# One plain chunk instead of two at the head of each feed-forward block, and a pair of chunks joined by TensorE in PSUM banks that ScalarE fills

## The chip, the cores and the metric

One core of one Trainium2 chip runs the whole program. TensorE multiplies into eight PSUM banks, VectorE, ScalarE and GpSimd work beside it, SP and GpSimd issue most of the DMAs. The metric is the device time of one execution in microseconds, before and after, over several runs.

## The reference

A trunk of two layers on two token batches (512 and 256 tokens, 768 in all, width 1024) with shared weights, in float32. Each layer adds half a feed-forward block, a token mixer (layer 0 a gated linear recurrence in both directions, layer 1 attention in a window of 128 tokens) and another half feed-forward block; a final norm closes it.

```python
def swiglu_ffn(x, w1, w2):
    gate, up = jnp.split(x @ w1, 2, axis=-1)
    return (jax.nn.silu(gate) * up) @ w2

for li in range(DEPTH):
    x = x + 0.5 * swiglu_ffn(rmsnorm(x, norm_g[li, 0]), ffn_w1[li, 0], ffn_w2[li, 0])
    h = rmsnorm(x, norm_g[li, 1])
    ...
    x = x + mix
    x = x + 0.5 * swiglu_ffn(rmsnorm(x, norm_g[li, 2]), ffn_w1[li, 1], ffn_w2[li, 1])
return rmsnorm(x, final_norm_g)
```

So there are four feed-forward blocks, f0 to f3. w1 is 1024 x 5632 (gate and up, 2816 columns each), w2 is 2816 x 1024.

## The kernel before, in words

**Number format.** Every float32 operand is split into a high part, rounded to the matmul format, and the low rest. A product is three matmuls: high by high, high by low, low by high. ScalarE makes the high part (L175, L208, L319), VectorE the low one by a subtraction (L176, L209, L320); in one product of each pair, p5, GpSimd makes the weight's low part (L209).

**Chunks.** The 2816 hidden columns are 22 chunks of 128. For a chunk the kernel needs the gate bank and the up bank for 768 tokens, and the tokens are handled in two halves of 384 (H). The inner size of 1024 is eight slices k, in two parts of four. The normalized, transposed tokens are held as operand tiles `b00`, `b10` (part 0 and 1 of half 0), `b01`, `b11` (half 1), split high and low.

**Plain chunks.** `up_plain` (L490) multiplies gate and up directly: for each of two banks and each half 8 k x 3 matmuls, through `mm3` (L312, its matmuls are L314 to L316), then silu on ScalarE (L504) and a multiplication on VectorE (L505).

**Pairs.** The other chunks take gate and up together as a 2 x 2 block matrix by 2 x 2 blocks of tokens, in seven products p1 to p7 instead of eight (the scheme of Strassen and Winograd). The weight blocks are a11, a12 (gate, part 0 and 1) and a21, a22 (up); sums of them are formed in place: a21 += a22 and a tile s3 = a21 + a11 by accumulating DMAs that GpSimd issues (L147), then "second" (a11 += a21) and "fourth" (a12 += a11) on VectorE (L215). The token side needs t1 to t4, differences of b00 to b11, made once a block by `sums` and `mix` (L420 to L442) and split by `put`. `FACTOR` names the token operand of each product: p1 takes b00, p2 b10, p3 b11, p4 t4, p5 t1, p6 t2, p7 t3. `product` (L508; the matmuls are L513) does 4 k x 3 matmuls into one bank; `up_pair` (L523) runs the seven into four banks a, b, c, d and joins them: ScalarE copies a and c out (L530, L533), VectorE does seven operations (L539 to L552), ScalarE the two silu.

**A block.** `ffn` (L601) works through `GROUPS` of four chunks. After four chunks the hidden values, in the same seven-product form (`gather`), go through `down_quad` (L556, matmuls L577), whose results are added to x on VectorE (L599). In the first group `PLAIN` chunks are plain, and between their matmuls stand calls of `run_later`, which run what is deferred: the two turns of half 1 (`turn`, transposes L385, copies L396, then `put`) and `sums`. Two remaining chunks are pairs whose hidden values go into the closing (the loop over `b` at the end of `ffn`, plain matmuls of 512 columns), where each block of 128 tokens is finished and normalized at once (`after_block`, `norm_block`) and half 0 is turned for the next stage. The stretch from a block's first plain matmul to its first product is called its opening here.

**Weights.** `plan_ffn` queues the weights. `load_next` issues the loads on SP's queue into `RAWBUFS` = 4 raw tiles; a pair also loads `s3` and starts its two accumulating DMAs on GpSimd's queue. `stage_next` makes one staged product (high and low) in the order `UP`; `WBUFS` = 8 staged tiles are there, a product of a pair takes one, a plain weight two. `ahead` stages as many as are free; `done` is release and ahead.

**Order.** A scheduler places the instructions: program order is the priority, and what is ready by its own cost model goes first on each engine; each engine then runs its list in order. `issue_after(x)` keeps what stands in its block behind x on the same engine.

Of the kernel before, what the change touches and what calls it, by code (L numbers as in the profile page):

```python
# [12 lines left out]
AF = mybir.ActivationFunctionType  # L13
# [3 lines left out]
P = 128  # L17
# [19 lines left out]
PLAIN = 2  # L37
# [6 lines left out]
UP = ("p1", "p7", "p2", "p5", "p4", "p6", "p3")  # L44
# [8 lines left out]
class Trunk:  # L53
    def __init__(self, ctx, tc, consts):
# [10 lines left out]
        self.uid = 0  # L65
        self.deferred = []
# [11 lines left out]
    def tmp(self, n, dt=F32):  # L78
        tag, bufs, size = ("tA", 8, TA) if n > TB else ("tB", 2, TB)
        t = self.tp.tile([P, size], dt, tag=tag, name=self.name(tag), bufs=bufs)  # L80
        return t[:, :n]

# [98 lines left out]
    def quad_steps(self, key, raws, srcs, order):  # L181
# [35 lines left out]
        behind = {"p5": "second", "p4": "fourth"} if up else {}  # L217
# [94 lines left out]
    def mm3(self, out, a, b, first, last):  # L312
# [3 lines left out]
        nc.tensor.matmul(out, a[1], b[0], start=False, stop=last)  # L316
# [122 lines left out]
    def sums(self):  # L439
        for kp in range(2):  # L440
            tiles = (self.tn[(i // 2, i % 2)][:, kp] for i in range(4))
            self.mix(*tiles, lambda name, src: self.put(name, kp, src))  # L442
# [27 lines left out]
    def plan_ffn(self, tag, w1, w2):  # L470
        def up(i):
# [4 lines left out]
            else:  # L476
                self.plan_quad((tag, i), (gate, up), (NC, P), UP)
# [12 lines left out]
    def up_plain(self, tag, j, half):  # L490
        pss = []
        for c in range(2):
            wh, wl = self.take((tag, j, c))
            ps = self.ps(H)
            for k in range(NC):
                b = self.operand(f"b{k // 4}{half}", k % 4)
                self.mm3(ps, (wh[:, k, :], wl[:, k, :]), b, k == 0, k == NC - 1)
                if half == 0 and k in (((), (2, 6)), ((3, 7), (3, 7)))[j][c]:
                    self.run_later()
            if half:  # L500
                self.done((tag, j, c))
            pss.append(ps)
        t = self.tmp(H)
        self.nc.scalar.activation(t, pss[0], AF.Silu)  # L504
        self.nc.vector.tensor_mul(t, t, pss[1])  # L505
        return t
# [16 lines left out]
    def up_pair(self, tag, j):  # L523
        nc = self.nc
        key = (tag, j)
        a, b, c, d = (self.ps(H) for _ in range(4))
        v, w, t = (self.tmp(H) for _ in range(3))
        p = lambda name, ps, first, last: self.product(key, name, FACTOR[name], ps, first, last)
        p("p1", a, True, False)
        nc.scalar.copy(v, a)  # L530
        self.ahead()
        p("p7", c, True, False)
        nc.scalar.copy(w, c)  # L533
        self.ahead()
        p("p2", a, False, True)
        nc.scalar.activation(a, a, AF.Silu)
        self.ahead()
        p("p5", d, True, False)
        nc.vector.tensor_sub(w, w, d)  # L539
        self.ahead()  # L540
        p("p4", c, False, True)
        p("p6", b, True, True)
        nc.vector.tensor_sub(v, v, b)
        nc.vector.tensor_sub(t, c, v)
        nc.vector.tensor_mul(t, t, a)  # L545
        yield t
        nc.vector.tensor_sub(w, w, v)
        self.ahead()
        p("p3", d, False, True)
        nc.vector.tensor_add(v, v, d)  # L550
        self.last_act = nc.scalar.activation(v, v, AF.Silu).ins
        self.last_dve = nc.vector.tensor_mul(w, v, w).ins  # L552
        yield w
        self.ahead()

    def down_quad(self, tag, g, hid):  # L556
        nc = self.nc
        cols = lambda b, c: self.x[b][:, c * 512 : (c + 1) * 512]
        if g == 0:
            for i in range(HB):  # L560
                x12, x21, x22 = cols(HB + i, 0), cols(i, 1), cols(HB + i, 1)
                nc.vector.tensor_add(x12, x12, x22)
                nc.vector.tensor_sub(x21, x21, x22)
# [37 lines left out]
    def ffn(self, tag, next_row):  # L601
        for g in range(GROUPS):
# [7 lines left out]
            def gather(ts, kp):  # L610
                self.mix(ts[0], ts[1], ts[2], ts[3], lambda name, src: put(name, src, kp))

            if g == 0:
                ts = {}
                for half in range(2):
# [944 lines left out]
```

## Time and profile before

| | before |
|---|---|
| time, median of 3 runs | 2768.38 us (2768.38 to 2769.55) |
| span of the profiled execution, first to last instruction | 2767.2 us |
| the profiled execution's own time by the page | the span; the median of the runs is 1.2 us longer |
| TensorE busy | 2745.0 us (99%), 15117 matmuls |
| VectorE busy | 2206.5 us (80%) |
| ScalarE busy | 1386.0 us (50%) |
| GpSimd busy | 453.0 us (16%) |
| mean granted TensorE clock | 0.999 |

The trace names instructions by engine (PE, PEld for weight loads, DVE for VectorE, ACT for ScalarE, POOL for GpSimd, SP) and by line of the kernel. The chain of waits follows the work that ended last back to what released it. In the groups, the numbers behind the bar are busy time, mean duration of one, and idle time just before them with what ended it. Durations of matmuls overlap: the distance from one to the next is read from a run of them in the chain. In a list in order of time the columns are start, duration, engine, line, operation, tiles; a bracket is idle time before it and what ended that.

### The profile page before, as it was taken

Reading aid. Unit: us, or ns where it says so; the run is one execution under the profiler, and the core shown is the slowest. Engines: PE = TensorE matmul, PEld = TensorE weight load, DVE = VectorE, ACT = ScalarE, POOL = GpSimd, SP = SyncE. Lnnn points to the kernel's source line nnn. Section 1 sums busy time; section 2 is a strip of 40 time slices with the busy share of each in tenths; the row PEclk is TensorE's granted clock in tenths of the full one; section 3 lists DMA queues with packets and bytes.
Section 4 is the critical chain, followed back from the end, with each engine's and each line's share of the span. In section 5 each row is a group of like instructions: output and inputs, shape, how many; then the busy total and the mean of one; then the engine's idle time right before and its main releaser. Section 6 shows DMA issues by size and latency. Waiting matters only on the chain.

```text
span 2767.2 us, 40933 instructions
## 1 busy us (share of the span) xinstructions
PE 2745.0 (99%) x15117; PEld 2554.8 (92%) x15117; DVE 2206.5 (80%) x3766; ACT 1386.0 (50%) x2589; POOL 453.0 (16%) x491
## 2 busy tenths in 40 slices
PE   8999999999999999999999999999999999999998
PEld 8999999989999889999999999999888889999998
DVE  8788788767887888788878887887847868788877
ACT  7344444634455675444445543444458855444443
POOL 2111121200000101211111121111105611211111
PEclk9999999999999999999999999999999999999999
DMA  6554554851122743655444355544424422655443
GB/s 172 130 125 114 126 140 124 227 161 39 39 62 66 205 119 78 143 134 131 115 117 121 78 145 134 126 119 118 130 73 111 89 69 73 145 134 130 114 118 107
DMA packets 352040, 325.22 MB, mean 118 GB/s; under 512 B 14216, under 2 KB 271200, under 8 KB 351840
## 3 DMA queue, kind: packets, MB, share of 16 engines
q1 hardware_dynamic: 303040, 224.56, 27.7%
q0 software_dynamic: 44496, 84.56, 17.4%
q10 hardware_dynamic: 4304, 13.49, 1.3%
q8 instruction: 118, 1.93, 0.3%
q14 instruction: 82, 0.67, 0.1%
HBM read 225.82 MB, written 15.73 MB: 87 GB/s over the span
## 4 chain that ended last, share of the span: by engine, by line
PE 96%; DVE 2%; ACT 1%; DMA 1%; issue 0%; DVEq 0%; POOL 0%; SPq 0%; ACTq 0%; POOLq 0%
PE ps L513 42%; PE ps L577 21%; PE ps L315 6%; PE ps L316 6%; PE ps L314 6%; PE ps L760 5%; PE ps L823 3%; PE ps L928 1%; PE ps L1414 1%; PE ps L904 1%; PE ps L385 1%; PE ps L1426 0%; PE ps L1376 0%; PE ps L1427 0%; PE ps L1377 0%; PE ps L1181 0%
## 5 line engine op out<-in xcount | busy, mean ns | idle before, releaser
L513 PE MATMUL ps<-big,w 128*128 128x384 f32 x6720 | 1169.3, 334 | 0.0
L513 PEld LDWEIGHTS ps<-big,w 128*128 128x128 f32 x6720 | 1165.9, 188 | 1.7 <-ACT tA L530 0.2
L208 ACT CAST w<-wr 128x512 fp32r<-128x512 f32 x600 | 415.8, 707 | 689.2 <-PE ps L513 274.9
L577 PE MATMUL ps<-w,big 128*128 128x512 f32 x2520 | 575.7, 390 | 0.0
L577 PEld LDWEIGHTS ps<-w,big 128*128 128x128 f32 x2520 | 472.7, 188 | 98.0 <-ACT big L319 0.4
L209 DVE TENSOR_TENSOR w<-wr,w 128x512 fp32r<-128x512 f32 (+1 forms) x520 | 438.0, 846 | 145.9 <-ACT w L208 123.9
L147 POOL DMA_DIRECT2D s<-wr x126 | 109.8, 878 | 1250.3 <-DMA s<-in_ffn_w_dram 432.0
L599 DVE SCALAR_TENSOR_TENSOR x<-ps,x 128x512 f32<-128x512 f32 x468 | 302.4, 686 | 10.1 <-PE ps L316 10.0
L314 PE MATMUL ps<-big,w 128*128 128x384 f32 x640 | 219.6, 345 | 1.2 <-ACT w L175 0.9
L315 PE MATMUL ps<-big,w 128*128 128x384 f32 x640 | 215.7, 337 | 0.7 <-DVE big L320 0.7
L316 PE MATMUL ps<-big,w 128*128 128x384 f32 x640 | 214.6, 335 | 0.0
L319 ACT CAST big<-tA 128x384 fp32r<-128x384 f32 x296 | 148.0, 513 | 115.4 <-DVE tA L545 37.0
L147 POOL DMA_DIRECT2D wr<-wr x109 | 94.9, 871 | 518.3 <-DMA wr<-in_ffn_w_dram 165.9
L760 PE MATMUL ps<-w,big 128*128 128x512 f32 x756 | 177.1, 392 | 0.1
L320 DVE TENSOR_TENSOR big<-tA,big 128x384 fp32r<-128x384 f32 x296 | 168.0, 578 | 6.7 <-ACT big L319 4.7
L209 POOL TENSOR_TENSOR w<-wr,w 128x512 fp32r<-128x512 f32 x80 | 137.4, 1718 | 197.8 <-ACT w L208 195.8
L760 PEld LDWEIGHTS ps<-w,big 128*128 128x128 f32 x756 | 140.6, 188 | 29.1 <-DVE w L320 0.6
L215 DVE TENSOR_TENSOR wr<-wr,wr 128x512 f32<-128x512 f32 (+1 forms) x120 | 123.3, 1027 | 25.9 <-issue 23.6
L314 PE MATMUL ps<-w,big 128*128 128x512 f32 x336 | 134.6, 401 | 0.1
L316 PE MATMUL ps<-w,big 128*128 128x512 f32 x336 | 131.8, 392 | 0.5 <-DVE big L400 0.5
L315 PE MATMUL ps<-w,big 128*128 128x512 f32 x336 | 131.8, 392 | 0.0
L315 PEld LDWEIGHTS ps<-big,w 128*128 128x128 f32 x640 | 120.6, 188 | 2.0 <-DVE big L320 1.7
(214 smaller groups left out, 3504.0 us busy)
## 6 DMA issues: line engine op xcount, KB each, us to landing
wr<-in_ffn_w_dram SPq DMA_DIRECT2D x264, 512.0 KB, 4.0
s<-wr POOLq DMA_DIRECT2D x126, 256.0 KB, 4.8
s<-in_ffn_w_dram SPq DMA_DIRECT2D x120, 256.0 KB, 3.2
wr<-wr POOLq DMA_DIRECT2D x80, 256.0 KB, 3.8
wr<-in_hg_w_in_dram SPq DMA_DIRECT2D x32, 512.0 KB, 3.9
wr<-wr POOLq DMA_DIRECT2D x29, 512.0 KB, 4.6
spill<-x ACTq DMA_DIRECT2D x12, 512.0 KB, 4.0
kept<-big POOLq DMA_DIRECT2D x8, 768.0 KB, 9.7
```

Of the source, the lines that this page charges most:

```text
L147: self.nc.gpsimd.dma_start(out, src, accum_op=ALU.add)
L208: nc.scalar.copy(h, src)
L209: (eng or nc.vector).tensor_sub(l, src, h.bitcast(F32))
L314: nc.tensor.matmul(out, a[0], b[0], start=first, stop=False)
L315: nc.tensor.matmul(out, a[0], b[1], start=False, stop=False)
L316: nc.tensor.matmul(out, a[1], b[0], start=False, stop=last)
L319: self.nc.scalar.copy(hi, src)
L320: self.nc.vector.tensor_sub(lo, src, hi.bitcast(F32))
L513: self.nc.tensor.matmul(ps, a[x], b[y], start=first and k == 0 and i == 0, stop=k == 3 and i == 2, skip_group_check=True,)
L577: nc.tensor.matmul(ps, a[x], w[y], start=name == chain and kp == 0 and q == 0, stop=kp == 1 and q == 2, skip_group_check=True,)
L599: self.nc.vector.scalar_tensor_tensor(x, ps, c, x, ALU.mult, ALU.add)
L760: nc.tensor.matmul(ps, x[:, sl], y, start=fresh and k == 0 and q == 0, stop=k == 3 and q == 2, skip_group_check=True,)
```

## The change

- `PLAIN` is 1: chunk 1 of each block becomes a pair. The groups stay five of four chunks, and the last two chunks stay pairs.
- The opening is put in a new order: the plain chunk's gate part 0 for half 0, p1 of chunk 1, up part 0, gate part 1, up part 1, p2 of chunk 1, then the plain chunk's half 1, then p5, p6, p3, p7 of chunk 1, p1 of chunk 2 and p4 of chunk 1. The plain parts of half 0 are kept in this order among themselves. The deferred steps stand behind gate part 1, up part 1 and p2. Chunk 1's weights are staged in the order `UP_OPEN`.
- A pair's sums are formed in PSUM: ScalarE writes -a into bank b before p6 adds to it, and b into bank c before p7 and p4 add to c. VectorE keeps four operations. The first such banks of a block are those that the plain chunk wrote (`wide`). In a pair half 1 is finished first and half 0 last.
- The weight's "second" is formed behind p1 and "fourth" behind p2.
- `sums` forms each token factor for both kp together, in the order t1, t2, t3, t4.
- The six additions of x ahead of the first `down_quad` are kept behind chunk 1's last VectorE operation.
- The closing starts with the first halves of three token blocks instead of two, and the staging of the next stage's weights that followed its last matmuls follows the whole loop.

```diff
-PLAIN = 2
+PLAIN = 1
...
-UP = ("p1", "p7", "p2", "p5", "p4", "p6", "p3")
+UP = ("p1", "p5", "p6", "p2", "p7", "p3", "p4")
+UP_OPEN = ("p1", "p2", "p5", "p6", "p3", "p7", "p4")
...
+    def seeded(self):
+        return self.wide.pop(0) if self.wide else self.ps(H)
...
-        behind = {"p5": "second", "p4": "fourth"} if up else {}
+        behind = {"p1": "second", "p2": "fourth"} if up else {}
...
     def sums(self):
-        for kp in range(2):
-            tiles = (self.tn[(i // 2, i % 2)][:, kp] for i in range(4))
-            self.mix(*tiles, lambda name, src: self.put(name, kp, src))
+        b11, b12, b21, b22 = (self.tn[(i // 2, i % 2)] for i in range(4))
+
+        def form(name, t, a, b):
+            for kp in range(2):
+                self.nc.vector.tensor_sub(t[:, kp], a[:, kp], b[:, kp])
+            return lambda: [self.put(name, kp, t[:, kp]) for kp in range(2)]
+
+        t3 = form("t3", b22, b12, b22)
+        form("t1", b12, b11, b12)()
+        form("t2", b11, b11, b22)()
+        t3()
+        form("t4", b21, b21, b11)()
...
+    def up_plain(self, tag, half, steps):
+        ps = [self.ps(H) for _ in range(2)]
+        t, last = self.tmp(H), None
+        for c, part in steps:
+            wh, wl = self.take((tag, 0, c))
+            with self.tc.issue_after(last) if last and not half else nullcontext():
+                for k in range(4 * part, 4 * part + 4):
+                    b = self.operand(f"b{part}{half}", k % 4)
+                    last = self.mm3(ps[c], (wh[:, k, :], wl[:, k, :]), b, k == 0, k == NC - 1).ins
+            if half and part:
+                self.done((tag, 0, c))
+            if part and not c:
+                self.nc.scalar.activation(t, ps[0], AF.Silu)
+            yield
+        self.nc.vector.tensor_mul(t, t, ps[1])
+        self.wide += ps
+        yield t
...
+    def up_first(self, tag, j, early=False):
+        a = self.ps(H)
+        self.product((tag, j), "p1", FACTOR["p1"], a, True, False)
+        b = self.tmp(H) if early else self.seeded()
+        self.nc.scalar.activation(b, a, AF.Copy, scale=-1.0)
+        self.ahead()
+        return a, b
+
+    def up_second(self, tag, j, a):
+        t = self.tmp(H)
+        self.product((tag, j), "p2", FACTOR["p2"], a, False, True)
+        self.nc.scalar.activation(t, a, AF.Silu)
+        self.ahead()
+        return t
+
+    def up_pair(self, tag, j, first=None, second=None, gap=None):
+        nc = self.nc
+        a, b = first or self.up_first(tag, j)
+        d = self.ps(H)
+        w = self.tmp(H)
+        p = lambda name, ps, first, last: self.product((tag, j), name, FACTOR[name], ps, first, last)
+
+        def third(v):
+            p("p3", d, False, True)
+            nc.vector.tensor_sub(v, d, v)
+            self.last_act = nc.scalar.activation(v, v, AF.Silu).ins
+            self.ahead()
+
+        p("p5", d, True, False)
+        nc.scalar.copy(w, d)
         self.ahead()
+        c = self.seeded()
+        if second:
+            v, b = b, self.ps(H)
+            p("p6", b, True, True)
+            nc.vector.tensor_add(v, b, v)
+            nc.scalar.copy(c, v)
+        else:
+            v = self.tmp(H)
+            p("p6", b, False, True)
+            nc.scalar.copy(c, b)
+            nc.scalar.copy(v, b)
         self.ahead()
+        if second:
+            t = second
+            third(v)
+        else:
+            t = self.up_second(tag, j, a)
+        p("p7", c, False, False)
+        nc.vector.tensor_sub(w, c, w)
         self.ahead()
+        if not second:
+            third(v)
+        nc.vector.tensor_mul(w, v, w)
+        yield 1, w
+        if gap:
+            gap()
         p("p4", c, False, True)
+        self.last_dve = nc.vector.tensor_mul(t, c, t).ins
+        yield 0, t
         self.ahead()
...
         if g == 0:
+            with self.tc.issue_after(self.begun):
+                for i in range(HB):
+                    x12, x21, x22 = cols(HB + i, 0), cols(i, 1), cols(HB + i, 1)
+                    nc.vector.tensor_add(x12, x12, x22)
+                    nc.vector.tensor_sub(x21, x21, x22)
...
                 if g == 0 and kp == 0:
+                    plain = self.up_plain(tag, 0, ((0, 0), (1, 0), (0, 1), (1, 1)))
+                    next(plain)
+                    first = self.up_first(tag, 1, True)
+                    next(plain)
+                    next(plain)
+                    self.run_later()
+                    next(plain)
+                    self.run_later()
+                    keep(0, 0, next(plain))
+                    second = self.up_second(tag, 1, first[0])
+                    self.run_later(len(self.deferred))
+                    *_, t = self.up_plain(tag, 1, ((0, 0), (0, 1), (1, 0), (1, 1)))
+                    keep(0, 1, t)
+                    opened = []
+                    for half, t in self.up_pair(tag, 1, first, second, lambda: opened.append(self.up_first(tag, 2))):
+                        keep(1, half, t)
+                else:
+                    for j in range(2):
+                        n = 4 * g + 2 * kp + j
+                        for half, t in self.up_pair(tag, n, opened[0] if n == 2 else None):
+                            keep(j, half, t)
                 gather(ts, kp)
+                if g == 0 and kp == 0:
+                    self.begun = self.last_dve
...
-                    self.done((tag, "last", c))
+                    self.release((tag, "last", c))
...
-            for i, k in (((0, 0), (1, 0), (0, 1)), ((1, 1),))[b] if b < 2 else ((b, 0), (b, 1)):
+            for i, k in (((0, 0), (1, 0), (2, 0), (0, 1)), ((1, 1),), ((2, 1),))[b] if b < 3 else ((b, 0), (b, 1)):
...
             self.after_block(b, next_row)
             if b >= 4:
                 self.run_later()
+        self.ahead()
```

79 lines of the change are left out of this document (10 added, 69 removed).

## The prediction

> **What bounds the kernel now.** I read the page's busy times and its chain of waits first, then the chain in order of time, then the busy time in windows.
>
> ```profile
> span 2767.2 us, 40933 instructions
> ...
> PE 2745.0 (99%) x15117; PEld 2554.8 (92%) x15117; DVE 2206.5 (80%) x3766; ACT 1386.0 (50%) x2589; POOL 453.0 (16%) x491
> ...
> PE 96%; DVE 2%; ACT 1%; DMA 1%; issue 0%; DVEq 0%; POOL 0%; SPq 0%; ACTq 0%; POOLq 0%
> ...
> L513 PE MATMUL ps<-big,w 128*128 128x384 f32 x6720 | 1169.3, 334 | 0.0
> ```
>
> ```profile
> 110.08 58.26 PE ps L513 x336
> 168.35 28.60 PE ps L577 x126
> ...
> 500.34 1.31 PE ps L385 x12
> ```
>
> TensorE sets the end: 96% of the chain, 99% busy, and no idle time before the 6720 matmuls of L513. The chain gives the prices. A 384-column matmul follows the last one after 58.26/336 = 173.4 ns (its 334 ns in the groups overlap), a 512-column one after 28.60/126 = 227 ns, a transpose after 1.31/12 = 109 ns. Only removed matmuls or removed holes can shorten this kernel; what moves among the other engines counts where it makes TensorE wait. Holes can be looked for in the four openings (first plain matmul to first product of L513) and at the very end:
>
> ```profile
> core 0: us, PE busy (x) PEld busy (x) DVE busy (x) ACT busy (x) POOL busy (x), PEclk, DMA share, GB/s
> 14.30:52.10 37.80, 36.87 (x219) 36.29 (x218) 37.80 (x54) 30.67 (x51) 10.54 (x5) 1.00 0.63 148
> 1025.90:1062.70 36.80, 36.42 (x216) 35.92 (x217) 33.02 (x44) 27.36 (x45) 6.14 (x3) 1.00 0.26 58
> 1516.00:1552.70 36.70, 36.64 (x219) 36.01 (x218) 33.24 (x44) 26.79 (x45) 4.48 (x3) 1.00 0.23 55
> 2271.80:2308.60 36.80, 36.71 (x220) 35.90 (x218) 32.10 (x42) 27.09 (x45) 6.14 (x3) 1.00 0.21 51
> ```
>
> An opening is 192 plain matmuls and 24 transposes, 192 x 0.1734 + 24 x 0.109 = 35.9 us. So f0's opening holds 37.8 - 35.9 = 1.9 us of holes, and the others 0.9, 0.8 and 0.9. In f0 VectorE is busy for all 37.80 us: a second limit lies close there.
>
> **Term 1, fewer matmuls.** A plain chunk is 2 banks x 2 halves x 8 k x 3 = 96 matmuls; a pair by seven products is 7 x 4 x 3 = 84. One chunk in each of four blocks changes over: 4 x 12 x 173.4 ns = 8.32 us less, all on TensorE and all on the path. [...]
>
> **Term 2, f0's opening.** The new order is gate half (12 matmuls), p1 of chunk 1 (12), up half (12), then the other two halves, p2, the plain chunk's second half, p5. The plain parts of half 0 are held in that order among themselves; p1 isn't. Both of its neighbours come late:
>
> ```profile
> 14.31 0.69 PE L314 MATMUL ps<-big,w 128*128 128x384 f32 x1
> ...
> 25.07 0.44 PE L314 MATMUL ps<-big,w 128*128 128x384 f32 x1 [0.93 <-ACT w L175]
> ```
>
> ```profile
> 13.64 4.29 DVE L393 SCALAR_TENSOR_TENSOR big<-ps,cols,big 128x384 fp32r<-128x384 f32 x8
> 17.84 1.22 DVE L176 TENSOR_TENSOR w<-wr,w 128x1024 fp32r<-128x1024 f32 x1
> ```
>
> ```profile
> 10.48 8.97 SPq L160 DMA_DIRECT2D wr<-in_ffn_w_dram  x4
> ```
>
> ```profile
> DMA to landing us min/median/max: 5.1/7.7/9.7
> ```
>
> ```profile
> L563 DVE TENSOR_TENSOR x<-x,x 128x512 f32<-128x512 f32 x3 | 2.1, 691 | 0.0
> L562 DVE TENSOR_TENSOR x<-x 128x512 f32<-128x512 f32 x3 | 2.0, 692 | 0.0
> ```
>
> These are TensorE and VectorE in order of time, SP's weight loads from 10.48 us on with the time to landing of this line's first six, and VectorE's groups in f0's opening.
>
> The gate half ends at 14.31 + 12 x 0.1734 = 16.4. The up half's low part is done by VectorE at 17.84 + 1.22 = 19.06, behind eight subtractions of L393. Two of its first three matmuls need only the high part, so TensorE waits 19.06 - 16.4 - 0.35 = 2.3 us. p1 can't fill this: its raw tile is the first of the four loads from 10.48 on, so it lands at about 18.2 by the median (15.6 to 20.2), and a cast and a subtraction (0.62 and 0.69, rows below) follow. If the planner puts p1 ahead of the up half, the hole is 18.2 + 1.3 - 16.4 = 3.1 us or, with the latest landing, 5.1. In exchange the present hole at 25.07, where chunk 1's plain weights come late, has no cause any more. VectorE's cover: six additions of x (L562 and L563, 0.69 each) are held back until chunk 1's last product and leave this stretch, 4.1 us; two plain low parts (2 x 1.22) go, three product parts and the two additions of the weight quad (5 x 0.69) come. That is 3.1 us less until t1, so VectorE isn't what makes t1 late here; the order of the turns is. Half 1's second turn moves from behind 45 to behind 72 matmuls. Its transposes end at 14.31 + 2.3 + 72 x 0.1734 + 2.6 = 31.7; by the steps of term 3, 3.3 + 5.7 us later, t1 is ready at 40.7 (43.2 with other work between), and wanted at 14.31 + 2.3 + 120 x 0.1734 + 2.6 = 40.0. Taken: 1.1 late, nearer the early end because p3 can fill in; 2.3 + 1.1 = 3.4 against 1.9 now, +1.5; bounds -1.9 (no hole left) and +6 (the late landing and the whole chain of t1 and t2).
>
> **Term 3, the other openings.** Now the first factor (t3, for p7) is wanted behind 204 matmuls; after the change t1 is wanted behind 120, t2 behind 132, b11 behind 144, t3 behind 156, t4 behind 180 (p1 of chunk 2 lies ahead of p4). Half 1's second turn moves from behind 45 to behind 60. The rows of f2's opening give the lag from its transposes to b11 and the length of the sums:
>
> ```profile
> 1526.55 0.82 PE L385 MATMUL ps<-ident_r,big 128*128 128x128 f32 x6
> ```
>
> ```profile
> 1528.88 1.83 DVE L320 TENSOR_TENSOR big<-big,big 128x768 fp32r<-128x768 f32 x2 [1.61 <-ACT big L319]
> 1530.62 0.95 DVE L422 TENSOR_TENSOR big<-big,big 128x768 f32<-128x768 f32 x1
> ```
>
> ```profile
> L320 DVE TENSOR_TENSOR big<-tA,big 128x384 fp32r<-128x384 f32 x296 | 168.0, 578 | 6.7 <-ACT big L319 4.7
> ```
>
> From the last transpose (1527.4) to both low parts of b11 (1530.7) are 3.3 us. After the change the transposes end at 1516.0 + 0.4 (half of today's hole) + 60 x 0.1734 + 2.6 = 1529.4, b11 is done at 1532.7, then come two subtractions for t3, two for t1 and t1's low parts, six at 0.95: 1538.4, or 1540.9 with one multiplication (0.55), one low part of the hidden tile (0.58) and two staged products (2 x 0.69) among them. p5 is wanted at 1516.0 + 0.4 + 120 x 0.1734 + 2.6 = 1539.8. So t1 is between 1.4 early and 1.1 late; t2 takes 3.8 us more where p5 lasts 2.1, and p3 can go ahead of p6 if the planner sees it. I take 0.5 an opening. Half of the present hole goes, because 36 matmuls instead of 24 now need b00 alone before b10. Three times 0.4 + 0.5 against 0.9 + 0.8 + 0.9: +0.1; bounds -2.6 and +6 (t1 and t2 late by 1.1 + 1.7 in each, less what goes).
>
> **Term 4, the pairs.** Work on TensorE's neighbours, by these rows:
>
> ```profile
> L539 DVE TENSOR_TENSOR tA<-tA,ps 128x384 f32<-128x384 f32 x80 | 44.1, 552 | 78.6 <-PE ps L513 78.6
> L543 DVE TENSOR_TENSOR tA<-tA,ps 128x384 f32<-128x384 f32 x80 | 44.1, 551 | 37.8 <-PE ps L513 37.6
> ...
> L530 ACT COPY tA<-ps 128x384 f32<-128x384 f32 x80 | 38.1, 477 | 27.4 <-PE ps L513 26.2
> ```
>
> ```profile
> DVE tA L543 <- PE ps L513: 37.6, 52, 3.6
> ```
>
> ```profile
> L208 ACT CAST w<-wr 128x512 fp32r<-128x512 f32 x480 | 291.3, 620 | 418.1 <-PE ps L513 209.0 <-DMA wr<-wr 68.9 <-DVE wr L215 58.5
> ...
> L209 DVE TENSOR_TENSOR w<-s,w 128x512 fp32r<-128x512 f32 x120 | 82.9, 691 | 16.0 <-ACT w L208 15.9
> ...
> L147 POOL DMA_DIRECT2D s<-wr x126 | 109.8, 878 | 1250.3 <-DMA s<-in_ffn_w_dram 432.0
> ...
> L209 POOL TENSOR_TENSOR w<-wr,w 128x512 fp32r<-128x512 f32 x80 | 137.4, 1718 | 197.8 <-ACT w L208 195.8
> ```
>
> VectorE goes from seven to four operations of 0.55 us a pair, ScalarE from four to six of 0.48 (b and c are filled). There are 84 pairs: 139 us less on VectorE, 81 more on ScalarE; both lie beside matmuls and are priced at nothing. The hand-overs are what counts. b is filled after p1 and added to by p6, with p5 (12 x 173.4 ns = 2.08 us) between; c is filled after p6 and added to by p7, with p2 between; c is read by VectorE after p7 and added to by p4, with p3 between. Each needs about 0.5 us plus the wait in the queue. Today's copy of a has the same cover, p7, and L513 shows no hole. So 0 is taken; the other end is the last rival. A converted chunk also costs each block 2 x 0.88 us of GpSimd for two accumulating transfers, one more 256 KB load on SP's queue and one low part on GpSimd (1.7 us); GpSimd is 16% busy, and the loads stand where the plain chunk's stood, in the same queues.
>
> **Term 5, closings and end.** The closing now starts with three blocks' first halves (6 matmuls, 1.36 us, more) before the second: cover for the last product, which feeds half 0 now. Blocks 0 and 1 come 1.36 us later, block 2 onward when they do today. At the very end VectorE has no gap left after block 2:
>
> ```profile
> 2750.63 0.69 DVE L599 SCALAR_TENSOR_TENSOR x<-ps,x 128x512 f32<-128x512 f32 x1 [1.35 <-PE ps L316]
> ...
> 2762.54 1.42 DVE L1305 SCALAR_TENSOR_TENSOR big<-x,stat,big 128x512 f32<-128x512 f32 x2
> ```
>
> Its 1.35 us of idle time takes up most of the delay; +0.3 there (0 to 1.36) and +0.1 for three norms. Staging for the next stage starts only after the closing; where it feeds a stage at once (heads after f0, kv after f2) +0.3 (0 to 2.4, two casts of 1.22 us' subtractions late).
>
> **Sum.** -8.32 + 1.5 + 0.1 + 0 + 0.4 + 0.3 = -6.0 us. Against the profiled span that is 2761.2. The median of the runs is 2768.38, 1.2 us above the span; I keep that distance: 2762.4.
>
> **Rivals.** (a) The factors eat the gain: t1 and t2 late in all four openings, or p1 ahead of the up half in f0. Terms 2 and 3 nearer their ends, +4.5 and +2, leave about 1 to 5 us of gain: 2763.4 to 2767.4, at 2765 in the middle. For it: f0's VectorE row has no idle time. Against it: t1 comes out level with its want. (b) Nothing is given back: the openings end without holes (-1.9 and -2.6): 2768.4 - 8.3 - 4 = about 2756 to 2760, at 2758.5. For it: 36 matmuls cover b10, and x's additions leave. Against: the up half's low part at 19.06. (c) Slower: TensorE waits at p4 for VectorE's read of c. It decides once that read ends more than 2.08 us after p7, that is, once 1.4 us of other work stands ahead of it (two staged subtractions). VectorE found its operand ready, and so was behind, in 28 of 80 cases of L543; if 29 of 84 pairs lose 0.69 us, that is +20 us: 2782. Against it: VectorE waits 78.6 us in all at L539, and loses 139 us of work. [...] That the change does not do what it says is no rival: the count of matmuls follows from the code.
>
> **Chances.** Forecast (2760.5 to 2763.4) 0.42, (a) 0.32, (b) 0.19, (c) 0.07. A measurement of this kernel can tell about 0.2%, 5.5 us, from no change: 2762.8. Faster takes (b) and most of the forecast's case, 0.50; the rest of it and (a) are the same, 0.43; slower 0.07. The range 2758 to 2767.4 leaves out (c) and the ends of (a) and (b).
>
> **What would show it.** Right: 48 matmuls fewer; L513 in runs of 173.4 ns with no idle time; in f0 a hole of some 2.3 us at 16.4 released by VectorE's L176 and none at 25; t1's wait under 1 us. Wrong: idle time before p5 or p6 put down to VectorE's split, a hole at p4 in many pairs, or a first product that waits for its load.

## The result and the profile after

The changed kernel takes 2850.45 us (median of 4 runs, 2848.47 to 2855.95) against 2768.49 for the kernel before (2768.38 to 2769.55): a ratio of 1.0299, 95% interval 1.0284 to 1.0314. It is 82 us slower, where 6 us faster was forecast. The page of the changed kernel, and its groups of TensorE instructions (busy time, mean ns of one, idle time just before them and what ended it):

```profile
span 2854.2 us, 40787 instructions
...
PE 2770.4 (97%) x15069; PEld 2560.9 (90%) x15069; DVE 2153.9 (75%) x3562; ACT 1449.5 (51%) x2779; POOL 501.9 (18%) x503
...
PE 73%; DMA 10%; DVE 8%; ACT 4%; issue 2%; POOL 2%; SPq 0%; POOLq 0%; DVEq 0%; ACTq 0%
```

```profile
L527 PE MATMUL ps<-big,w 128*128 128x384 f32 x7056 | 1251.3, 338 | 40.5 <-POOL w L214 26.7 <-ACT w L213 8.6 <-DVE tA L586 3.0
L621 PE MATMUL ps<-w,big 128*128 128x512 f32 x2520 | 586.6, 393 | 18.9 <-DVE x L643 18.9
```

The 48 matmuls are gone (15117 to 15069), VectorE has 52.6 us less to do, ScalarE 63.5 more. But TensorE no longer carries the chain alone: 73% of it, where it was 96%. Before, the products of pairs showed no idle time (their row is in the prediction), nor did the down products, by the same view of the kernel before:

```profile
L577 PE MATMUL ps<-w,big 128*128 128x512 f32 x2520 | 575.7, 390 | 0.0
```

Now they have 40.5 and 18.9 us, under three names: a low part made by GpSimd (L214), a cast by ScalarE (L213), and additions to x by VectorE (L643). The three holes have their places. First the opening of f1, in order of time, without the weight loads:

```profile
1052.81 1.52 ACT L401 ACTIVATE big<-ps,cols 128x384 f32<-128x384 f32 x3
...
1053.39 0.34 PE L321 MATMUL ps<-big,w 128*128 128x384 f32 x1
1054.20 1.59 ACT L324 CAST big<-big 128x768 fp32r<-128x768 f32 x2
...
1055.66 1.69 ACT L213 CAST w<-wr 128x512 fp32r<-128x512 f32 x3
1056.36 0.79 PE L527 MATMUL ps<-big,w 128*128 128x384 f32 x2 [2.64 <-ACT w L213]
...
1058.55 2.59 PE L527 MATMUL ps<-big,w 128*128 128x384 f32 x10
```

**Hole 1.** The gate half is done at 1053.4; the next thing in TensorE's list is p1 of chunk 1, and its weight is cast only at 1055.66, behind the turn's copies and casts on ScalarE. f2 has the same hole (2.62 us), f0 one of 3.31 us, f3 none. A bracket counts idle time from the modelled end of the last matmul; read from start to start, a hole is 0.16 us longer. The expectations below count in that way, with 2.8 and 3.5 us here and 6.7 to 7.1 for the next one.

**Hole 2**, 27 us later, in GpSimd's, VectorE's and TensorE's own lists:

```profile
1080.15 9.95 POOL L214 TENSOR_TENSOR w<-wr,w 128x512 fp32r<-128x512 f32 x1 [1.79 <-ACT w L213]
```

```profile
1079.87 0.95 DVE L449 TENSOR_TENSOR big<-big,big 128x768 f32<-128x768 f32 x1
1080.74 0.95 DVE L325 TENSOR_TENSOR big<-big,big 128x768 fp32r<-128x768 f32 x1
1081.61 0.95 DVE L449 TENSOR_TENSOR big<-big,big 128x768 f32<-128x768 f32 x1
1082.47 2.69 DVE L325 TENSOR_TENSOR big<-big,big 128x768 fp32r<-128x768 f32 x3
...
1089.35 1.29 DVE L220 TENSOR_TENSOR wr<-wr,wr 128x512 f32<-128x512 f32 x1
```

```profile
1090.15 8.55 PE L527 MATMUL ps<-big,w 128*128 128x384 f32 x37 [6.59 <-POOL w L214]
```

```profile
L214 POOL TENSOR_TENSOR w<-wr,w x84: 1282/1416/11281, 27.5 to 2803.5; 128x512 fp32r<-128x512 f32 x84
```

The low part of p5 of chunk 2 takes GpSimd 9.95 us, where the median of its 84 is 1.42 (last row: minimum, median, maximum in ns). For nearly all of that time VectorE runs subtractions that read two tiles of SBUF, the factors and low parts, without a gap and at their usual durations (0.95 us for 128x768). That product stands ahead of chunk 1's p6 and p3 in TensorE's list, so TensorE stands still for 6.6 us with other work behind it. All four openings have this hole, of 6.58 to 6.92 us.

**Hole 3**, at the start of the down products:

```profile
1131.81 1.75 PE L621 MATMUL ps<-w,big 128*128 128x512 f32 x7
...
1132.60 1.22 DVE L214 TENSOR_TENSOR w<-wr,w 128x1024 fp32r<-128x1024 f32 x1
...
1134.67 0.68 DVE L643 SCALAR_TENSOR_TENSOR x<-ps,x 128x512 f32<-128x512 f32 x1
...
1135.41 4.91 PE L621 MATMUL ps<-w,big 128*128 128x512 f32 x20 [1.85 <-DVE x L643]
```

Between p1 and p2 of a down product VectorE must add p1's bank to x. It gets there at 1134.67, behind results of the last pair and a low part, and TensorE waits 1.85 us.

**And behind holes 1 and 2 TensorE is slow.** In the first fence the five matmuls from 1056.95 on start 0.32 us apart, where 0.173 is usual. The windows of f1's opening show the granted clock (PEclk) around holes 1 and 2:

```profile
core 0: us, PE busy (x) PEld busy (x) DVE busy (x) ACT busy (x) POOL busy (x), PEclk, DMA share, GB/s
1045.00:1053.00 8.00, 7.24 (x45) 6.20 (x44) 6.24 (x12) 7.78 (x17) 1.73 (x2) 1.00 0.62 130
1056.30:1060.00 3.70, 3.64 (x12) 3.64 (x13) 3.67 (x5) 1.21 (x4) 1.82 (x1) 0.54 0.00 0
1066.00:1080.00 14.00, 14.00 (x87) 13.97 (x86) 11.32 (x15) 11.36 (x20) 0.88 (x1) 1.00 0.16 36
1090.60:1094.00 3.40, 3.40 (x12) 3.40 (x12) 0.60 (x2) 0.00 (x0) 0.90 (x1) 0.50 0.14 30
```

Behind each the clock is about half for some 3.5 us (0.54 over 3.70 us, 0.50 over 3.40). In the changed kernel 122 matmuls stand at a granted clock under 0.8, with the next one over 60 ns late and no idle time between; they cost 20.0 us. The kernel before has none (mean granted clock 0.990 against 0.999).

The profiled execution is 87.0 us longer than that of the kernel before (2854.2 against 2767.2), and from start to start this can be added up: holes 68.6 us more (that is over the 59.4 of the two rows, by 0.16 us a hole and by a few holes at other lines), half clock 20.0, delays with under 0.15 us of idle time each 6.3, less 8.3 for the 48 matmuls: 86.6.

### The profile page after: what moved, and what is told of

Read it like the earlier page. It is cut to its first block, busy times and chain, and to the rows that moved or that the text cites. A ratio compares the mean times of both kernels' runs of the same rounds, so it can differ in the third digit from the quotient of the medians.

```text
span 2854.2 us, 40787 instructions
## 1 busy us (share of the span) xinstructions
PE 2770.4 (97%) x15069; PEld 2560.9 (90%) x15069; DVE 2153.9 (75%) x3562; ACT 1449.5 (51%) x2779; POOL 501.9 (18%) x503
## 3 DMA queue, kind: packets, MB, share of 16 engines
q1 hardware_dynamic: 305152, 225.61, 26.7%
## 4 chain that ended last, share of the span: by engine, by line
PE 73%; DMA 10%; DVE 8%; ACT 4%; issue 2%; POOL 2%; SPq 0%; POOLq 0%; DVEq 0%; ACTq 0%
PE ps L527 29%; PE ps L621 18%; PE ps L319 5%; PE ps L320 5%; PE ps L321 5%; DMA wr<-in_ffn_w_dram 5%; PE ps L817 4%; DMA wr<-wr 4%; PE ps L880 3%; DVE w L214 3%; ACT w L213 2%; POOL w L214 1%; DVE big L325 1%; ACT big L324 1%; PE ps L985 1%
## 5 line engine op out<-in xcount | busy, mean ns | idle before, releaser
L527 PE MATMUL ps<-big,w 128*128 128x384 f32 x7056 | 1251.3, 338 | 40.5 <-POOL w L214 26.7
L527 PEld LDWEIGHTS ps<-big,w 128*128 128x128 f32 x7056 | 1235.1, 190 | 52.8 <-POOL w L214 28.0
L213 ACT CAST w<-wr 128x512 fp32r<-128x512 f32 (+1 forms) x624 | 429.6, 704 | 595.9 <-DVE wr L220 242.6
L214 DVE TENSOR_TENSOR w<-wr,w 128x512 fp32r<-128x512 f32 (+1 forms) x540 | 455.1, 851 | 209.1 <-ACT w L213 152.1
L621 PE MATMUL ps<-w,big 128*128 128x512 f32 x2520 | 586.6, 393 | 18.9 <-DVE x L643 18.9
L643 DVE SCALAR_TENSOR_TENSOR x<-ps,x 128x512 f32<-128x512 f32 x468 | 306.0, 682 | 16.8 <-PE ps L321 13.3
L214 POOL TENSOR_TENSOR w<-wr,w 128x512 fp32r<-128x512 f32 x84 | 172.7, 2056 | 311.3 <-ACT w L213 300.1
L319 PE MATMUL ps<-big,w 128*128 128x384 f32 x512 | 178.3, 349 | 1.8 <-ACT big L324 1.0
L152 POOL DMA_DIRECT2D wr<-wr x113 | 104.7, 927 | 411.8 <-DMA wr<-in_ffn_w_dram 173.3
L325 DVE TENSOR_TENSOR big<-tA,big 128x384 fp32r<-128x384 f32 x296 | 160.5, 553 | 21.2 <-ACT big L324 18.5
L320 PE MATMUL ps<-big,w 128*128 128x384 f32 x512 | 173.5, 339 | 1.9 <-DVE big L325 1.9
L321 PE MATMUL ps<-big,w 128*128 128x384 f32 x512 | 172.6, 337 | 0.0
L220 DVE TENSOR_TENSOR wr<-wr,wr 128x512 f32<-128x512 f32 (+1 forms) x124 | 127.2, 1026 | 40.6 <-DMA wr<-wr 32.6
L586 DVE TENSOR_TENSOR tA<-ps,tA 128x384 f32<-128x384 f32 x84 | 46.6, 555 | 77.9 <-PE ps L527 77.9
```

The source lines that it names most:

```text
L152: self.nc.gpsimd.dma_start(out, src, accum_op=ALU.add)
L213: nc.scalar.copy(h, src)
L214: (eng or nc.vector).tensor_sub(l, src, h.bitcast(F32))
L319: nc.tensor.matmul(out, a[0], b[0], start=first, stop=False)
L320: nc.tensor.matmul(out, a[0], b[1], start=False, stop=False)
L321: return nc.tensor.matmul(out, a[1], b[0], start=False, stop=last)
```

## The experiments

Twelve kernels, each timed against the kernel before in the same series (2768.6 to 2769.2 us there). "From" is the kernel that was edited.

| run | from | median us | ratio to before, 95% interval |
|---|---|---|---|
| e1_low_vector | after | 2824.41 | 1.0204 (1.0188 to 1.0219) |
| e2_p5_behind_p4 | after | 2823.17 | 1.0197 (1.0181 to 1.0212) |
| e3_closing_done | after | 2848.74 | 1.0288 (1.0272 to 1.0303) |
| e6_p1_behind_up | after | 2841.54 | 1.0255 (1.0238 to 1.0272) |
| e4_new_opening_old_pairs | after | 2815.60 | 1.0168 (1.0153 to 1.0183) |
| e5_old_opening_new_pairs | before | 2799.35 | 1.0112 (1.0095 to 1.0129) |
| e5b_whole_banks | e5 | 2801.14 | 1.0114 (1.0099 to 1.0129) |
| e7_down_p7_third | e5b | 2785.61 | 1.0057 (1.0042 to 1.0072) |
| e8_four_mends | after | 2804.02 | 1.0130 (1.0113 to 1.0147) |
| e9_old_pairs_mended | e4 | 2807.78 | 1.0141 (1.0126 to 1.0156) |
| e10_no_sums | e9 | 2787.72 | 1.0068 (1.0053 to 1.0083) |
| e9b_old_down | e9 | 2800.50 | 1.0113 (1.0096 to 1.0130) |

### Opening or pairs?

e4 keeps the new opening and takes the old joining, the old order of products and no early p1 for every pair behind chunk 1; e5 is the kernel before with only the joining and the order of a pair's products changed.

```diff
 # e4
-UP = ("p1", "p5", "p6", "p2", "p7", "p3", "p4")
+UP = ("p1", "p7", "p2", "p5", "p4", "p6", "p3")
...
-                        for half, t in self.up_pair(tag, n, opened[0] if n == 2 else None):
+                        for half, t in self.up_old(tag, n):
 # e5, from before: up_pair, UP and the order of the weight's sums as after the change
```

> The new opening and one plain chunk, but every pair behind chunk 1 is joined as before (VectorE's seven operations, the old order of products and of the weight's sums). Theory P (the new pairs cost about 29 us at the starts of the down products, 17 holes of 1.2 us and slow matmuls behind them): 2821 us or less, as chunk 2's p1 is not drawn ahead any more either, so part of the openings' holes can go too: 2785 to 2821 us. Rival O (the opening carries the whole loss, and the holes at the down products are those of the opening handed on): 2845 to 2855 us.

> The kernel before with two plain chunks, its old opening and its old closing, but with the new way of joining a pair and the new order of a pair's products. Theory P: the time before plus the holes at the down products, 2768 + 29 = 2797 us, with idle time of over 1 us at the first down products. Rival O: no such holes without the new opening, 2768 us within 5 us.

e4 is 46.9 us over the kernel before, e5 30.6: together 77.5 of the 82. So there are two losses, nearly independent, and theory P holds in both runs. (In e4 GpSimd's low part still makes holes of 4.1 us in f2 and f3 alone, so its opening isn't quite that of the changed kernel.) In e5 the first pairs of a block take other banks than the changed kernel does, and its outputs moved as if some of ScalarE's fills were lost there (by 0.43 of their size, last section); e5b gives those pairs the plain chunk's banks and does the same work:

```diff
 # e5b, in the plain chunk of e5
         self.nc.vector.tensor_mul(t, t, pss[1])
+        if half:
+            self.wide += pss
```

> The kernel before with the new way of joining pairs, as in the run with the old opening and the new pairs; the banks that ScalarE fills in the first two pairs of a block are now those that the plain chunks wrote, as in the changed kernel. The work is the same: 2799 us within 4. In the earlier run those fills were lost where the bank had last been written by transposes of 128 columns; here the sums should come out whole.

2801.14, 1.8 above e5: the time of e5 stands, and the new pairs alone cost 32 us.

### The pairs: what is late at the down products

The same place, the first down products of f0, in the kernel before and in e5:

```profile
163.08 1.05 ACT L208 CAST w<-wr 128x1024 fp32r<-128x1024 f32 x1 [2.54 <-DMA wr<-wr]
...
168.19 7.00 PE L577 MATMUL ps<-w,big 128*128 128x512 f32 x30
...
170.93 0.68 DVE L599 SCALAR_TENSOR_TENSOR x<-ps,x 128x512 f32<-128x512 f32 x1
```

```profile
168.39 2.00 ACT L208 CAST w<-wr 128x1024 fp32r<-128x1024 f32 x2 [4.26 <-DMA wr<-wr]
...
169.48 1.23 DVE L209 TENSOR_TENSOR w<-wr,w 128x1024 fp32r<-128x1024 f32 x1 [3.26 <-ACT w L208]
169.62 4.28 PE L606 MATMUL ps<-w,big 128*128 128x512 f32 x18
...
171.21 0.53 ACT L548 ACTIVATE tA<-tA 128x384 f32<-128x384 f32 x1 [0.81 <-DVE tA L547]
...
175.46 0.69 DVE L628 SCALAR_TENSOR_TENSOR x<-ps,x 128x512 f32<-128x512 f32 x1
...
176.20 3.97 PE L606 MATMUL ps<-w,big 128*128 128x512 f32 x16 [2.30 <-DVE x L628]
```

The cast of the down weight a21 waits for an accumulating transfer. It was released at 163.08, 5 us ahead of the down products; now at 168.39, 1.2 us ahead of them. ScalarE's list stands at it for 4.26 us and VectorE's for 3.26; the silu and the last pair's results are queued behind and then come all together, and the first addition to x is 5.8 us after the start of the down products instead of 2.7. e7 moves that cast one product later:

```diff
-DOWN = ("p1", "p2", "p5", "p4", "p7", "p6", "p3")
+DOWN = ("p1", "p2", "p7", "p5", "p4", "p6", "p3")
```

> As the run beside it (old opening, new pairs, whole banks), with one change: in the down products p7 stands third and p5 fourth, so that the cast of a21, which waits for an accumulating transfer that lands at 168.33, stands one product (18 matmuls, 4.1 us) later in ScalarE's list. Theory L (ScalarE's list stands at that cast for 4.26 us, silu and VectorE's results behind it, and so the first addition to x comes late): the holes of the first down products (12.0 us, 3.2 in small ones, some 5 of slow matmuls) go, 15 to 20 us less, 2780 to 2784 us. Rival R (both halves' results fall into the last 4 us ahead of the down products, whatever ScalarE waits for): 2794 to 2799 us.

2785.61, 15.5 us less. The down products in the groups, of e5b and of e7:

```profile
L519 PE MATMUL ps<-big,w 128*128 128x384 f32 x6720 | 1175.7, 335 | 4.9 <-ACT ps L569 3.3 <-DVE tA L578 1.5
L612 PE MATMUL ps<-w,big 128*128 128x512 f32 x2520 | 581.6, 391 | 14.7 <-DVE x L634 14.6
```

```profile
L519 PE MATMUL ps<-big,w 128*128 128x384 f32 x6720 | 1175.2, 335 | 4.7 <-ACT ps L569 3.5 <-DVE tA L578 1.1
L612 PE MATMUL ps<-w,big 128*128 128x512 f32 x2520 | 578.1, 390 | 0.0
```

All 14.7 us of idle time at the down products are gone: theory L. Over the 20 down products the transfer lands 5.2 us ahead of them in the kernel before, 3.0 in e5b and 3.2 in e7 (medians). So the place shown is a late one, 2 us later is usual, and in e7 the holes went without the transfer coming earlier. Why it lands later wasn't tried; at the place shown its last load was issued 1.0 us later and landed 4.3 us later, beside another accumulating transfer that had been done by then before.

In the profiled executions e7 is 17.0 us over the kernel before. Holes make 9.1 of that; 4.7 us of their idle time are at the products, nearly all of it four waits of 1.05 to 1.15 us, one in the first pair of each block (three for ScalarE's fill of c, f0's for VectorE's read of it). Delays with under 0.15 us of idle time each make 7.6, and no run here splits them further.

### The openings: GpSimd's low part and TensorE's list

```diff
 # e1
-split(name, own[name], nc.gpsimd if up and name == "p5" else None)
+split(name, own[name], nc.gpsimd if up and name == "p5" and key[1] > 2 else None)
...
 # e2; last_pe is the last matmul of the product before
-        p("p5", d, True, False)
+        with self.tc.issue_after(self.last_pe) if j == 2 else nullcontext():
+            p("p5", d, True, False)
```

> In chunks 1 and 2 of each block the low part of p5's weight is made by VectorE instead of GpSimd; nothing else changes. Theory G (the four holes of 6.7 to 7.1 us in the openings of the changed kernel come from GpSimd's subtraction, stretched to 9.95 us beside VectorE): the holes go, and the slow matmuls behind them too; about 4 x (7 + 2) = 36 us less than the changed kernel, some 2814 us. Rival H (the holes come from chunk 2's p5 standing too early in TensorE's list, whoever makes its weight): VectorE is as busy there, its subtraction comes as late behind its queue, and over half of the hole stays: 2835 to 2850 us.

> Chunk 2's p5 is kept behind chunk 1's p4 on TensorE, so that a late low part of its weight has 48 matmuls (8.3 us) more time; GpSimd still makes it. Theory H (the place in the list is half of the cause): the wait for GpSimd goes, 2814 to 2820 us. Rival: the products that now stand ahead (p6, p3, p7 of chunk 1) wait for their own factors, as VectorE still makes them, and the idle time is only put down to VectorE instead: 2835 to 2850 us.

e1 is 26.0 us under the changed kernel and e2 27.3; both lie between their theory and their rival. In e2 GpSimd is as slow as ever, and it hurts no more; the products of e1 and, with GpSimd's own row, of e2:

```profile
L527 PE MATMUL ps<-big,w 128*128 128x384 f32 x7056 | 1245.9, 336 | 21.7 <-DVE w L214 9.5 <-ACT w L213 8.0 <-DVE tA L586 2.2
```

```profile
L527 PE MATMUL ps<-big,w 128*128 128x384 f32 x7056 | 1246.9, 336 | 29.0 <-DVE w L214 9.2 <-ACT w L213 8.6 <-ACT ps L574 4.3
```

```profile
L214 POOL TENSOR_TENSOR w<-wr,w x84: 1283/1488/11304, 27.3 to 2771.2; 128x512 fp32r<-128x512 f32 x84
```

So the loss needs both: a low part that takes 10 us, and a product that stands in the list as if it took 1.4. Taking away either ends TensorE's wait for GpSimd, and e1 gives 26.0 us for it, not the 36 of theory G. In both the first thing that TensorE waits for is then VectorE's low part of a weight (9.5 and 9.2 us), which stands behind the factors. In e2 the idle time at the down products fell too, from 18.9 to 8.2 us, so its 27.3 are not the price of this hole alone; that was not followed up.

### The openings: p1

```diff
 # e3
-                    self.release((tag, "last", c))
+                    self.done((tag, "last", c))
...
-        self.ahead()
...
 # e6
                     next(plain)
-                    first = self.up_first(tag, 1, True)
                     next(plain)
+                    first = self.up_first(tag, 1, True)
                     next(plain)
```

> The changed kernel, but the next stage's weights are staged within the closing, as before the change. Theory S (p1's cast in the openings of f1 and f2 comes late because its staging now stands behind the whole closing and the turn): the two holes of 2.8 us ahead of p1 and the slow matmuls behind them (1.6 us each) go, 8.8 us less than the changed kernel, some 2842 us. Rival (p1 is late for its load or for VectorE's part, which the closing does not set): within 3 us of 2850.

> The changed kernel, but p1 of chunk 1 stands behind the up half instead of ahead of it, 12 matmuls or 2.1 us later. Theory S (the holes ahead of p1, 3.5 us in f0 and 2.8 in f1 and f2, are a first product that was set too early): in f1 and f2 0.7 us is left of each and the slow matmuls behind them go; in f0 the up half's own low part still costs some 2.3 us; 8 to 9 us less than the changed kernel, some 2842 us. Rival: the waits only move to the next product, within 3 us of 2850.

e3 came out 1.7 us under the changed kernel, inside the spread of both (2845.1 to 2853.5 here). f2's hole went, f1's stayed as it was, here in order of time in e3:

```profile
1054.02 1.69 ACT L213 CAST w<-wr 128x512 fp32r<-128x512 f32 x3
...
1054.72 0.62 PE L527 MATMUL ps<-big,w 128*128 128x384 f32 x2 [2.62 <-ACT w L213]
```

So when the closing stages does not explain f1's hole, and the time doesn't show that f2's was worth anything; my theory on it falls. e6 gives 8.9 us, as expected, and in its row no cast is named any more:

```profile
L527 PE MATMUL ps<-big,w 128*128 128x384 f32 x7056 | 1245.0, 336 | 28.6 <-POOL w L214 20.4 <-DVE tA L586 3.0 <-DVE big L325 2.5
```

That the size fits is partly luck. GpSimd's share fell too, from 26.7 to 20.4: f0's hole of 6.92 us is gone, since VectorE happened to leave a gap there (last section), while other waits grew. The casts ahead of p1 held 8.6 us of idle time, but what they are worth alone, e6 doesn't show.

### Do they add up, and what is left?

e8 puts e1, e2, e6 and e7's order of the down products into the changed kernel. e9 puts e1, e6 and e7's order into e4 (old pairs), e9b is e9 with the old order of the down products, and e10 is e9 without the eight subtractions that form the factors:

```diff
 # e10, in sums
         def form(name, t, a, b):
-            for kp in range(2):
-                self.nc.vector.tensor_sub(t[:, kp], a[:, kp], b[:, kp])
             return lambda: [self.put(name, kp, t[:, kp]) for kp in range(2)]
```

> The changed kernel with four mends together: chunk 2's p5 behind chunk 1's p4, its and chunk 1's low part of p5 on VectorE, p1 of chunk 1 behind the up half, p7 third in the down products. Theory (three separate causes: the late low part of p5, 27 us; p1 too early, 9 us; the late cast ahead of the down products, 15.5 us): they add up, 2850.5 - 51.5 = 2799 us, 4 either way. Rival (VectorE's queue in the openings is one cause behind all of them, and what one mend frees the next wait takes): 2812 us or more.

> The new opening with the old pairs behind it, and p1 of chunk 1 behind the up half, p5's low part on VectorE in chunks 1 and 2, p7 third in the down products. From 2815.6: p1 9 us less; GpSimd's hole of 4.3 us in f2 and f3 down to VectorE's 2.3, 5 us less with slow matmuls; the three holes of 2.1 us at the first down products with the slow matmuls behind them, 10.8 us less: 2791 us, 4 either way. What stays over 2769 is then VectorE's work on the factors in the openings; if the openings were mended by this, it would come to 2772 or less.

> As the run with the old pairs and three mends, but the down products keep their order (p5 third, p7 fifth). In that run ten of the down products lost 1.40 us each to an addition to x, 14 us that no run with the old order of the down products showed. Theory D (with the old pairs the old order of the down products is the right one; p7 third asks for t3 before VectorE has it): the 14 us go, and the three holes of 2.1 us at the first down products of f1 to f3 come back with some 4.5 us of slow matmuls: 2804 us, or 2794 if these three were handed on from the opening and don't come back. Rival (the 1.40 us belong to the new opening): within 3 us of 2808.

> As the run beside it (new opening, old pairs, three mends), but the eight subtractions that form the token factors t1 to t4 of a block are left out of VectorE's queue (the factors are then wrong and so are the outputs; all else is done). Theory V (in the new opening VectorE has more to do than TensorE's products cover, and t1, t2 and the staged low parts stand behind each other): 7 us of VectorE's time go from each opening, and the holes of 2.3 us with the slow matmuls behind them and most of the holes of 0.8 us too: 16 to 22 us less than the run beside it. Rival (the order of the products alone makes them wait): within 5 us of the run beside it.

e8: 46.4 us less, of 51.5 by addition; it lies between the two theories. In the main the causes are separate. The 5 us that are missing are not split: f0's GpSimd hole is counted twice in the 51.5 (in the 27 and in e6's 8.9), and waits for VectorE lead its row:

```profile
L527 PE MATMUL ps<-big,w 128*128 128x384 f32 x7056 | 1244.5, 336 | 20.0 <-DVE w L214 9.4 <-DVE tA L587 4.7 <-DVE big L325 4.2
L622 PE MATMUL ps<-w,big 128*128 128x512 f32 x2520 | 577.9, 391 | 0.0
```

e9 missed its expectation by 17 us: p7 third in the down products, which helps the new pairs, hurts the old ones, ten times 1.40 us (from start to start). e9b takes it back and is 7.3 us faster, between its two cases: the ten waits are gone, and four at the first down products of the blocks are back. Rows of e9, of e9b (its down products alone) and of e10:

```profile
L527 PE MATMUL ps<-big,w 128*128 128x384 f32 x7056 | 1238.8, 336 | 10.6 <-DVE w L214 7.8 <-DVE big L325 2.8
L654 PE MATMUL ps<-w,big 128*128 128x512 f32 x2520 | 579.5, 390 | 12.4 <-DVE x L676 12.4
```

```profile
L654 PE MATMUL ps<-w,big 128*128 128x512 f32 x2520 | 580.0, 391 | 6.5 <-DVE x L676 6.5
```

```profile
L525 PE MATMUL ps<-big,w 128*128 128x384 f32 x7056 | 1229.9, 334 | 0.0
L652 PE MATMUL ps<-w,big 128*128 128x512 f32 x2520 | 579.6, 391 | 12.4 <-DVE x L674 12.4
```

e10 is 20.1 us under e9, and the products wait for nothing: theory V. The new opening asks VectorE for about 5 us per block more than the products cover, and taking away 7 us (8 x 0.95, overlapping a little) ends it. In e9's opening of f1 VectorE works from 1060.74 to the end of the hole at 1078.8 without a gap, as theory V has it. But in the 7 us ahead of that it sat idle for 4.7 us, behind the plain chunk's matmuls and the turn's casts, and in e10 t1's low part needs fewer of the turned tiles too. So an earlier turn of half 1 is a rival cure that no run here tried.

That cost of 20 us is larger than the gain of 8.3, so no order of the same work that was tried beats the kernel before. e10 itself stays 19.1 us over it. Ten waits of 1.40 us make 14.0 of that; with the 8.3 us saved, some 13 us more stay that no run here splits.

## Why the prediction was wrong

The sum was -6.0 us, the result +82; the range ended at 2767.4.

- **Term 1 (-8.32) was right**: 48 matmuls fewer, at the same distance (median from start to start 173 ns in both kernels).
- **Term 2 (f0's opening, +1.5)** named the case that came, p1 ahead of the up half with a hole of 3.1 us, and then took the other. The hole is 3.31 us with slow matmuls behind it. In f1 and f2 (2.64 and 2.62 us) the same wait was not priced at all, since there I looked at factors and not at p1's weight. Together that is 8.6 us of idle time; e6's gain of 8.9 holds another hole too.
- **Term 3 (the other openings, +0.1; at most +6)** failed at its step on VectorE: t1 and t2 were set against TensorE's want with two staged products between, as if the low parts of chunk 1's other weights came in gaps. They stand behind the factors in the same queue. By e10 that is 20 us over four openings, f0's among them, in the kernel of e9.
- **Term 4 (pairs and GpSimd, 0)** holds the two steps that cost most. "one low part on GpSimd (1.7 us); GpSimd is 16% busy" used a mean over the whole span for a stage in which VectorE runs two-input subtractions without a gap; the low part takes 10 us there, 26 us by e1. The trace before already had one such, in f0's opening (the maximum in this row, 8.12 us):

```profile
L209 POOL TENSOR_TENSOR w<-wr,w x80: 1289/1547/8121, 45.3 to 2721.3; 128x512 fp32r<-128x512 f32 x80
```

  The other step is "both lie beside matmuls and are priced at nothing". It asked only for the hand-overs inside a pair, which were mis-sized by little (4.7 us in e7's row). Not asked was what the new order of products and weight sums moves in the queues ahead of the down products: a transfer that lands some 2 us later, ScalarE's list that stands at its cast, 15.5 us by e7. The new pairs cost 32 us where 0 was taken.
- **Term 5 (closing, +0.7)** can't be told from nothing by e3 (1.7 us within the spread).
- **Rival (c)**, the only slower one, named a mechanism that is there but small: TensorE's wait for VectorE's read of c is 3.0 us in the changed kernel's row (0.75 us once a block), not 20. The loss has other places. Of the signs listed as "wrong", one came nearly as written, a first product that waits, though for its cast. Another came in f0 alone, where the opening's third product waits 1.21 us for VectorE's low part of a token factor. Holes 2 and 3, which wait for GpSimd and for additions to x, were on no list.
- **No term held a price for a hole's aftermath**: 20.0 us lost in the changed kernel's 122 matmuls at a granted clock under 0.8.

## What to carry to other kernels

Read a duration from the stage where the work will stand, with its maximum, not from the mean over the span: a GpSimd subtraction of 1.4 us took 10 beside VectorE's two-input work without a gap. When products are reordered, follow each in-order list across the next stage's start, above all a cast that waits for a transfer (15.5 us by e7). Saved TensorE time is worth only what the other engines' queues in that stage can still cover (8.3 us were saved here, and without the factors in VectorE's queue e10 was 20.1 us shorter), and a hole may cost over half as much again in slow matmuls (hole 1: 2.64 us idle, then 3.70 us at a granted clock of 0.54, 1.7 us lost).

## What the runs showed of the hardware

**GpSimd beside VectorE.** In hole 2 GpSimd's subtraction began in the middle of one of VectorE's (1080.15 in 1079.87 to 1080.82). VectorE's next ones, begun after it but without a gap, kept their 0.95 us while it took 9.95. It ended at 1090.1, beside the one operation of VectorE that was stretched for its part (L220, 1.29 us, where the shortest of its kind take 0.68). Where GpSimd began first, it was the other way round, as here in f0 of the changed kernel:

```profile
162.91 1.28 POOL L214 TENSOR_TENSOR w<-wr,w 128x512 fp32r<-128x512 f32 x1 [0.61 <-ACT w L213]
```

```profile
162.94 1.67 DVE L428 TENSOR_TENSOR tA<-tA,tA 128x384 f32<-128x384 f32 x1
```

GpSimd, 0.03 us ahead, kept its 1.28 us; VectorE's subtraction took 1.67, where the 24 of this line that met no GpSimd subtraction take 0.55. This line has 16 such places. In e6's opening of f0 VectorE left a gap of 0.39 us (47.56 to 47.95): GpSimd's subtraction, begun at 47.27, took 1.45 us there, not the 11.28 of the changed kernel, and VectorE's next operation 1.58 instead of 0.95. So in these places the operation that was running kept its pace, and GpSimd's 9.95 and 11.28 us came beside operations of VectorE without a gap; no run varies the gap, or the two inputs of these operations, by itself.

**Half clock after short holes.** Behind hole 1 (2.64 us) the granted clock was 0.54 over 3.70 us, and behind a hole of 1.82 us at f0's first down products 0.56 over 3.90 us, 1.7 us lost each. It is not certain: behind hole 3 (1.85 us) it was 1.00 from 1135.40 to 1139.00, and in e3 f1's hole of 2.62 us was followed by a full clock, in this window:

```profile
1054.70:1058.00 3.30, 3.28 (x19) 3.23 (x20) 3.30 (x4) 1.01 (x2) 1.83 (x1) 1.00 0.00 0
```

So the length of a hole alone does not decide it: of 2.64 and 2.62 us, and of 1.82 and 1.85 us, the first had a clock near half behind it and the second, in these windows, a full one. What decides, no run shows.

**Filled banks.** In e5, the first pairs behind a turn took banks last written by transposes of 128 columns, and the outputs moved by 0.43 of their size; with the plain chunk's banks, written over all 384 columns, e5b's sums came out whole. The two runs show that the choice of bank decides; that in e5 a product replaced ScalarE's fill where it was to add to it, and that it was for the transposes, is argued from the program.
